# A streaming-encoder block on eight cores: the gate product in bf16 parts, masks made on chip, a finer last block, and head buffers moved

## The chip, the cores and the metric

One Trainium2 chip, all eight cores. Each core works on one of the eight batch elements, with no communication. The time is device microseconds of the slowest core. A program on all eight cores has a slow state in some executions (one die, or both, at a lower granted clock).

TensorE is the matmul engine, VectorE, ScalarE and GpSimd the three elementwise engines. SBUF is the on-chip memory that holds the operands, PSUM the one that TensorE writes its products to (`PS<-SB` in the lines below), in banks; an eviction is the instruction of another engine that reads a product out of PSUM. In the profile's lines they are PE (PEld for its weight loads), DVE, ACT and POOL; SP issues DMAs.

## The reference

For each batch element, x is 2048 tokens by 2048 channels, in float32. Cut to what matters here:

```
h   = rmsnorm(x) * (1 + sc1) + sh1                 # sc1, sh1, ... from c @ w_ada
gk  = log_sigmoid((gk_low @ w_gk2) + b_gk2) / 16   # gk_low: 16 channels of h @ w_in
...                                                # two chunked gated recurrences: 8 heads A, 4 heads B
x   = x + gt1 * (merge of both @ w_o)
h   = rmsnorm(x) * (1 + sc2) + sh2
x   = x + gt2 * ((silu(h @ w_g) * (h @ w_u)) @ w_ffn_out)
out = rmsnorm(x) * final_norm_w
```

The kernel holds channels on partitions and tokens along the free dimension, so the sum of squares over channels is a TensorE product with a matrix of constants, and the final scaling of a token is a multiplication with a tile that is the same on every partition.

## The kernel before

It treats the 2048 tokens in two halves of 1024. A small list scheduler orders all operations with hand-written costs, and each engine then runs its operations in that fixed order. The parts that the change touches:

```
# the gate product of a B head: one float32 product for each 512 tokens
mm([lambda e: e.matmul(p.ap, wgk2.ap[:, i*128:(i+1)*128], gkl[hf].ap, start=True, stop=True)], ...)

# buffers of the heads. Z = 140 KB; the output tiles xres[0..7] lie at Z .. Z+32 KB
r_v  = [sb(194*KB, 4096, BF16), sb(184*KB, 4096, BF16)]
r_B1 = ring(Z + 6*KB, 2, 1024, BF16)
r_B4 = ring(Z + 10*KB, 4, 1024, BF16)     # silu of the output gate
r_rs = ring(202*KB, 2, 512, F32)

# masks: 128 + 4 x 512 float32 columns, by five DMAs in the start
for t_, c0, s_ in ((ident, 0, 2), (m64, 128, 3), (m128, 640, 4), (cm64, 1152, 5), (cm128, 1664, 6)): ...

# the end of the second feed-forward product, for one 128-channel chunk fc
stt(x, p, gt2, x, ALU.mult, ALU.add)                    # VectorE: x += gt2 * psum
act(t_, x, AF.Square)                                   # ScalarE
padd(acc3, acc3, t_)  or  tt(acc3, acc3, t_, ALU.add)   # GpSimd in blocks of 256 (fc < 14), else VectorE
# ... once all 16 chunks of a block are done
norm_finish(acc3, rs3, hf)                              # one float32 product, then Ln and Exp on ScalarE
for fc in range(16):
    stt(x, x, final_norm_w[fc], rs3, ALU.mult, ALU.mult)   # VectorE, then a store

# the last half works its output in blocks
for hf in (0, (512, 256), (768, 256)):                  # (first token, tokens); 0 is 512 tokens
```

## Time and profile before

| | before |
|---|---|
| fast runs | 3772.95 and 3776.08 us |
| slow runs | 3907.97 and 3942.62 us |
| profiled run, span of each core | 3754.0 to 3770.3 us |
| granted TensorE clock of the cores | 0.983 to 0.988 |

The busy line of the profile (busy time, share of the span, instructions; the page that the prediction read has 97% for TensorE, with some hundred matmul records fewer):

```profile
PE 3678.2 (98%) x18414; PEld 1706.8 (45%) x18414; DVE 1334.7 (35%) x2246; ACT 880.1 (23%) x1266; POOL 379.8 (10%) x709
```

TensorE is the limit. What the other engines do costs time only where TensorE has to wait, at the start, or after its last matmul. Four places matter.

The gate product, in the timeline of TensorE (columns of all timeline fences: start, duration, engine, line and operation, operands, and in brackets the idle time before the first instruction of the group and what ended it). Two records are one product, as there are 32 records for 16 float32 products; the last line is two products.

```profile
417.22 1.02 PE L695 MATMUL PS<-SB 128*128 128x512 f32 x2
...
449.29 1.94 PE L695 MATMUL PS<-SB 128*128 128x512 f32 x4
```

The turn from the first half to the second. TensorE stops for 5.66 us: ScalarE could not write the silu of the gate until a store of output had read the same bytes.

```profile
1969.23 7.07 PE L643 MATMUL PS<-SB 128*128 128x512 bf16 x32
...
1980.53 1.29 DVE L380 TENSOR_TENSOR SB<-SB 128x512 bf16<-128x512 bf16 x2 [4.51 <-DMA outT<-SB]
1981.21 1.08 ACT L376 ACTIVATE SB<-PS 128x512 bf16<-128x512 f32 x2 [10.98 <-DMA outT<-SB]
...
1981.96 22.95 PE L643 MATMUL PS<-SB 128*128 128x512 bf16 x96 [5.66 <-ACT SB L376]
```

The start. TensorE makes modulation columns from w_ada_c as it lands; five mask loads (the fence shows four) are issued among the last of them.

```profile
119.86 2.11 POOL L417 DMA_DIRECT2D SB<-cst  x4 [0.64 <-ACT SB L376]
...
147.34 0.54 PE L546 MATMUL PS<-SB 128*128 128x1 bf16 x16 [1.12 <-DMA SB<-w_ada_c]
...
151.93 0.56 PE L546 MATMUL PS<-SB 128*128 128x1 bf16 x16 [4.04 <-DMA SB<-w_ada_c]
```

The end. The list of 128x256 matmuls runs from 3716 us on. The 16 multiplications of the first block of 256 stand in a row on VectorE (7.95 us), the evictions behind them wait, and TensorE stops for 1.80 us. After the last dense matmul (3754.5 us) come GpSimd's additions, the norm product, 16 multiplications and the last store, 15.8 us in all.

```profile
3716.35 19.38 PE L451 MATMUL PS<-SB 128*128 128x256 bf16 x176
...
3739.84 7.95 DVE L400 SCALAR_TENSOR_TENSOR SB<-SB 128x256 f32<-128x256 f32 x16
...
3748.33 6.16 PE L451 MATMUL PS<-SB 128*128 128x256 bf16 x55 [1.80 <-DVE SB L400]
...
3758.47 1.19 PE L508 MATMUL PS<-SB 128*128 128x256 f32 x2 [3.98 <-DVE SB L380]
...
3760.75 6.42 DVE L400 SCALAR_TENSOR_TENSOR SB<-SB 128x256 f32<-128x256 f32 x16 [2.43 <-ACT SB L376]
```

### The profile page before, as it was taken

To read this page: it belongs to the slowest core of one execution; us is meant where nothing else is said; L and a number is where in the kernel's file an instruction comes from. 1 tells how busy PE (TensorE), PEld (TensorE's weight loads), DVE (VectorE), ACT (ScalarE), POOL (GpSimd) and SP (SyncE) were. 2 spreads that over 40 slices of the span, in tenths; PEclk is the share of its full clock that TensorE was granted. 3 is DMA by queue.
4 is the path that set the end of the run, shared out by engine and by line. 5 is a ranking of instruction groups with operands and counts; after the bars stand their busy time and mean duration, and the time that the engine had idled before them with its cause. 6 is when DMAs were issued, how large, how long until landed. Compare 5 with 4: busy or idle time off the path is not lost.

```text
span 3770.1 us, 46917 instructions; the slowest of 8 cores (3754.0 to 3770.3 us)
## 1 busy us (share of the span) xinstructions
PE 3657.4 (97%) x18062; PEld 1707.6 (45%) x18414; DVE 1336.0 (35%) x2246; ACT 880.1 (23%) x1266; POOL 379.8 (10%) x709
## 2 busy tenths in 40 slices
PE   6799999999999999999999999999999999999998
PEld 2344444444444444444444444444444444444445
DVE  2267755532553112231165554321243120211116
ACT  3466323111330000220136643311123000000002
POOL 1111001111011001000000000011101000100002
PEclk7699999999999999999999999999999999999999
DMA  9956558977486545555464433345646454544542
GB/s 195 153 96 108 88 90 129 167 140 141 83 168 116 85 66 86 113 110 88 74 135 100 68 68 68 59 87 99 119 96 116 71 85 71 83 75 69 85 69 90
DMA packets 124540, 377.82 MB, mean 100 GB/s; under 512 B 13601, under 2 KB 20641, under 8 KB 124321
## 3 DMA queue, kind: packets, MB, share of 16 engines
q0 software_dynamic: 97776, 315.44, 50.9%
q1 hardware_dynamic: 26546, 59.36, 5.4%
q8 instruction: 151, 2.47, 0.3%
q14 instruction: 67, 0.55, 0.1%
HBM read 673.35 MB, written 16.78 MB: 183 GB/s over the span
## 4 chain that ended last, share of the span: by engine, by line
PE 92%; DMA 5%; DVE 1%; issue 1%; ACT 1%; SPq 0%; POOL 0%; DVEq 0%; POOLq 0%; ACTq 0%
PE PS L451 82%; PE PS L643 6%; DMA SB<-w_ada_c 1%; DMA SB<-xT 1%; DMA SB<-w_fi_l 1%; DMA SB<-w_ada_l 1%; DVE SB L400 1%; DVE SB L380 1%; ACT SB L376 0%; PE PS L756 0%; PE PS L562 0%; DMA outT<-SB 0%; PE PS L773 0%; PE PS L778 0%; PE PS L695 0%
## 5 line engine op out<-in xcount | busy, mean ns | idle before, releaser
L451 PE MATMUL PS<-SB 128*128 128x512 bf16 (+1 forms) x14869 | 3243.6, 377 | 25.7 <-DMA SB<-w_fi_l 3.2
L451 PEld LDWEIGHTS PS<-SB 128*128 128x128 bf16 x15184 | 1481.4, 98 | 1755.0 <-issue 23.9
L376 ACT ACTIVATE SB<-PS 128x512 f32<-128x512 f32 (+2 forms) x585 | 351.1, 613 | 2266.0 <-PE PS L451 2019.1
L380 DVE TENSOR_TENSOR SB<-PS,SB 128x512 bf16<-128x512 f32 (+1 forms) x256 | 168.2, 657 | 1060.6 <-PE PS L451 947.8
L400 DVE SCALAR_TENSOR_TENSOR SB<-PS,SB 128x512 f32<-128x512 f32 (+2 forms) x416 | 299.6, 727 | 464.3 <-PE PS L451 400.2
L376 ACT ACTIVATE SB<-SB 128x512 f32<-128x512 f32 (+5 forms) x519 | 339.9, 689 | 464.2 <-DVE SB L400 262.2
L380 DVE TENSOR_TENSOR SB<-SB 128x512 f32<-128x512 f32 (+6 forms) x501 | 303.5, 624 | 195.8 <-ACT SB L376 122.3
L400 DVE SCALAR_TENSOR_TENSOR SB<-SB,PS 128x128 f32<-128x128 f32 (+2 forms) x448 | 206.5, 461 | 440.5 <-PE PS L451 400.3
L400 DVE SCALAR_TENSOR_TENSOR SB<-SB 128x2048 bf16<-128x2048 bf16 (+3 forms) x208 | 240.0, 1179 | 62.1 <-DMA SB<-w_ada_l 52.7
L643 PE MATMUL PS<-SB 128*128 128x512 bf16 x999 | 230.1, 382 | 7.5 <-ACT SB L376 5.8
L376 ACT ACT_TABLE_LOAD x146 | 187.3, 1283 | 121.8 <-PE PS L451 75.5
L417 POOL DMA_DIRECT2D SB<-w_fi_l x176 | 92.9, 528 | 1001.3 <-PE PS L451 951.5
L417 POOL DMA_DIRECT2D SB<-w_in_l x144 | 76.1, 529 | 879.8 <-PE PS L451 548.7
L643 PEld LDWEIGHTS PS<-SB 128*128 128x128 bf16 x1024 | 98.7, 98 | 121.2 <-issue 10.0
L417 POOL DMA_DIRECT2D SB<-w_fo_l x128 | 67.6, 528 | 605.0 <-PE PS L451 580.5
L408 DVE CAST SB<-PS 128x512 bf16<-128x512 f32 x64 | 44.1, 690 | 86.5 <-PE PS L643 83.4
L562 PE MATMUL PS<-SB 128*128 128x512 bf16 x86 | 40.8, 610 | 34.0 <-ACT SB L376 33.2
L614 DVE TENSOR_TENSOR_SCAN SB<-SB 128x512 f32<-128x512 bf16 x48 | 58.1, 1218 | 31.6 <-ACT SB L376 31.5
L417 POOL DMA_DIRECT2D SB<-w_ada_l x64 | 33.9, 529 | 172.3 <-PE PS L451 58.3
L525 PE MATMUL PS<-SB 128*128 128x512 f32 x64 | 33.1, 672 | 10.3 <-ACT SB L376 10.3
L408 DVE CAST SB<-SB 128x512 bf16<-128x512 f32 x96 | 40.4, 421 | 0.0
L417 POOL DMA_DIRECT2D SB<-w_v_l x32 | 16.9, 529 | 180.5 <-PE PS L451 99.1
(42 smaller groups left out, 492.9 us busy)
## 6 DMA issues: line engine op xcount, KB each, us to landing
SB<-w_fi_l POOLq DMA_DIRECT2D x176, 512.0 KB, 5.8
SB<-w_in_l POOLq DMA_DIRECT2D x144, 512.0 KB, 6.2
SB<-w_fo_l POOLq DMA_DIRECT2D x128, 352.0 KB, 4.5
SB<-xT SPq DMA_DIRECT2D x64, 512.0 KB, 10.4
SB<-w_ada_l POOLq DMA_DIRECT2D x64, 512.0 KB, 8.4
SB<-w_ada_c POOLq DMA_DIRECT2D x32, 512.0 KB, 19.0
SB<-w_v_l POOLq DMA_DIRECT2D x32, 512.0 KB, 6.1
SB<-w_o_l POOLq DMA_DIRECT2D x32, 512.0 KB, 10.2
```

The lines of the kernel that those rows point to most:

```text
L376: return g.op('act', lambda e: e.activation(out=out.ap, in_=in_.ap, func=func, **kw), reads=[in_] + aps, writes=[out], cost=cost, key=key, ...
L380: return g.op('dve', lambda e: e.tensor_tensor(out=outap if outap is not None else out.ap, in0=in0ap if in0ap is not None else in0.ap, in1 ...
L400: return g.op('dve', lambda e: e.scalar_tensor_tensor(out=out.ap, in0=in0.ap, scalar=v, in1=in1.ap, op0=op0, op1=op1, **kw), reads=[in0, i ...
L408: g.op('dve', lambda e: e.tensor_copy(out=outap if outap is not None else out.ap, in_=inap if inap is not None else in_.ap), reads=[in_], ...
L417: return g.op(q, lambda e: e.dma_start(out=oa, in_=ia), reads=list(reads), writes=list(writes), dsem=sem, nbytes=nbytes, cost=0.6, key=key ...
L451: fns = [(lambda e, k=k: e.matmul(p.ap, w.ap[:, k * 128:(k + 1) * 128], H(acts[k], hf).ap, start=(k == 0), stop=(k == nk - 1))) for k in ks]
L525: mm([lambda e, k=k, hf=hf, q=q: e.matmul(nb[hf].ap, onesD.ap, H(q, hf).ap, start=(k == 0), stop=(k == 15))], [onesD, H(q, hf)], [nb[hf]], ...
L562: mm([lambda e, p=p, j=j, hf=hf, kc=kc: e.matmul(p.ap, ws[j].ap[:, kc * 128:(kc + 1) * 128], H(hT[kc], hf).ap, start=(kc == 0), stop=(kc = ...
L614: g.op('dve', lambda e: e.tensor_tensor_scan(out=dst.ap, data0=mask.ap, data1=src.ap, initial=0.0, op0=ALU.mult, op1=ALU.add), reads=[mask ...
L643: fns = [(lambda e, i=i, j=j, p=p, tb=tb: e.matmul(p.ap, hT[4 * i + j].ap[:, tb * 128:(tb + 1) * 128], ws[i].ap[:, j * 512:(j + 1) * 512], ...
```

## The change

Its intent: shorten TensorE's float32 work (each float32 value of the gate product is split into a bf16 value and a bf16 remainder, and two bf16 products replace one float32 product), take bytes out of the start, take the wait for a store out of the turn, and shorten what follows the last matmul. The core of the diff, with cuts marked by "...":

```diff
-        gkl = [sb(MG + 26 * KB, 512, F32), sb(MG + 28 * KB, 512, F32)]
+        wg_hi, wg_lo = sb(MG + 25 * KB, 512, BF16), sb(MG + 26 * KB, 512, BF16)
+        gkl = [sb(MG + 27 * KB, 512, BF16), sb(MG + 28 * KB, 512, BF16)]    # rows of high and of low parts
...
-                mm([... e.matmul(p.ap, wgk2.ap[:, i * 128:(i + 1) * 128], gkl[hf].ap, start=True, stop=True)],
+                mm([... e.matmul(p.ap, w_.ap[:, i * 128:(i + 1) * 128], gkl[hf].ap, start=(n_ == 0), stop=(n_ == 1))
+                    for n_, w_ in enumerate((wg_hi, wg_lo))], ...)
...
-        r_v = [sb(194 * KB, 4096, BF16), sb(184 * KB, 4096, BF16)]
+        r_v = [sb(194 * KB, 4096, BF16), sb(Z + 10 * KB, 4096, BF16)]
-        r_B1 = ring(Z + 6 * KB, 2, 1024, BF16)
-        r_B4 = ring(Z + 10 * KB, 4, 1024, BF16)
+        r_B1 = ring(202 * KB, 2, 1024, BF16)
+        r_B4 = ring(184 * KB, 4, 1024, BF16)
-        r_rs = ring(202 * KB, 2, 512, F32)
+        r_rs = ring(Z + 6 * KB, 2, 512, F32)
...
-    cst_d = din("cst", [128, 128 + 4 * 512])
+    cst_d = din("cst", [128, 384])          # cm64, cm128 by memset; m64, m128 broadcast over four blocks
...
+                    elif q == 3:            # the last half
+                        a_ = H((acc3, acc4)[fc % 2], hf)
+                        t_ = q3().cols(0, width(hf)) if fc > 1 else a_
+                        act(t_, x, AF.Square)
+                        act(x, x, AF.Copy, scale=sm(SM_NF + fc), key=2.5)      # final_norm_w, on ScalarE
+                        if fc > 1:          # odd chunks on GpSimd, even ones on VectorE
+                            (padd if fc % 2 else lambda o_, a, b: tt(o_, a, b, ALU.add))(a_, a_, t_)
...
+                norm_finish([acc3, acc4], rs3, hf)                             # two float32 products
+                for f0 in ((4, 12, 0, 8) if n == 512 else (12, 0, 4, 8)):      # four chunks at a time
+                    pl = f0 == 12 or (n == 512 and f0 == 4)
+                    ...
+                    g.op('pool' if pl else 'dve', lambda e, ...: e.tensor_tensor(out=base, in0=base, in1=rsb, op=ALU.mult), ...)
...
-                    for hf in (0, (512, 256), (768, 256)):
+                    for hf in (0, (512, 256), (768, 128), (896, 128)):
```

## The prediction

> **What bounds it now.** TensorE: in the busy table 97% of 3770 us. Its 15,000 dense 128x512 bf16 matmuls stand 0.216 us apart in the timeline, at a granted clock of 0.985. Its waits by cause sum to only about 21 us after 157 us; before that it waits for xT, then w_ada_c. So three things pay: less matmul time, the start, the tail after the last matmul. VectorE (35%), ScalarE (23%) and GpSimd (10%) have room everywhere but at the end.
>
> **What the change does.**
>
> 1. Gate product. In the timeline a pair of float32 records of the gate matmul takes 0.86 to 0.91 us; 32 records are 16 products. Two bf16 products take 2 x 0.216 = 0.43 us. Saving 0.46 x 16 = about 7 us on TensorE, where it has no idle. "TensorE: Matmul & The Clock Gate" (the Trainium skill, Weight-path perf modes) ties fast weight load to non-float32 types; the trace agrees (loads of 190 ns in float32, 98 in bf16).
>
> 2. Head buffers. At the turn of the two 1024-token halves the timeline shows TensorE idle from 1976.3 to 1982.0 us: two silu evictions waited 11 us for an output DMA, since their target overlays output tiles. Afterwards nothing in the first head's front does. Saving 5 to 5.7 us.
>
> 3. Masks. Five cst loads (1.1 MB of HBM reads) are issued at 120 to 123 us amid the last w_ada_c loads, for which TensorE waits until 151.9. From 126.3 to 151.8 about 8 MB landed, 0.32 MB/us; 0.92 MB less is about 3 us.
>
> 4. Tail. The last dense matmul ends near 3754.5, the span at 3770.3: 15.8 us of GpSimd additions to 3757, norm, 16 multiplications of 128x256 on VectorE (6.4 us), last store (3 us). TensorE also stood 1.8 us at 3746.5, behind the multiplications of the block before. After, for 128 tokens, estimated from the durations shown: eviction, square, addition 1.5; norm 1.7 to 2; three multiplications of 128x512 on VectorE 2.1; last store 2.5 to 3: 8 to 9 us. 128-wide matmuls stand 0.056 us apart, so two blocks of 128 (19.7 us) cost TensorE little more than one of 256 (19.2). Against it: norm sums take two float32 products (+0.9, +0.5, +0.3 us), and in the 128 blocks ScalarE (two instructions of an estimated 0.31 us per 0.62 us) and VectorE (about 9.5 of 9.9 us) are at their limit, an estimated lag of 1 to 2 us. Net 5 to 7 us.
>
> The broadcast mask costs VectorE the same 0.69 us; the silu ring, cut to two, is reused every 6.9 us only.
>
> **Sum.** 7 + 5.5 + 3 + 6 = about 21 us, 0.6%. From fast runs of 3773 to 3776: **3753 us**, range 3743 to 3764. Faster by over 2%: 0.01; within 2%: 0.97; slower: 0.02.
>
> **What would show each step.** Gate: 32 bf16 records 0.216 us apart. Turn: no TensorE idle over 1 us after the second half's first front, no wait for an output DMA. Masks: the last w_ada_c wait ends near 149 us. Tail: 8 to 10 us from last dense matmul to end, no stall in the 256 block.
>
> **What would make it wrong.** GpSimd's wide multiplications (4 x 512 columns, an estimated 4 to 6 us each) block its additions and, through the ring of squares, ScalarE and the evictions. VectorE is slowed beside GpSimd (its 128x512 multiplications went from 0.74 to 0.82-0.99 us). The start may be limited by the ring of eight w_ada_c tiles, not bytes: then term 3 is nothing. The list schedule shifts, adding small stalls. A slow-state run (3908 was seen) as the median.

## The result, and the profile after

| | before | after |
|---|---|---|
| fast runs | 3772.95, 3776.08 us | 3762.99 to 3764.37 us (four) |
| slow runs | 3907.97, 3942.62 us | 3891.29, 3911.76 us |
| profiled run, span of each core | 3754.0 to 3770.3 us | 3747.3 to 3763.2 us |

The ratio is 0.9972, with a 95% interval from 0.9948 to 0.9996: about 10.6 us less, half of the 21 us that the prediction summed. A ratio here is the mean time of one kernel's fast runs over that of the other's of the same rounds, so it is not quite the ratio of medians. Of the four fast runs one lies at the very top of the predicted range of 3743 to 3764 and three just above it.

Cores differ by up to 20 us within one execution, so one core's trace is a poor yardstick for single terms. The next table gives the mean over all eight cores of each profiled execution, worked out from the times in the traces: the start of the first value product (after the start-up), the first 128x256 dense matmul (where the last 512 tokens begin to be worked in smaller blocks), the end of the last dense matmul, and the span.

| mean of 8 cores, us | before | after | difference |
|---|---|---|---|
| start to the first value product | 176.3 | 173.5 | -2.8 |
| from there to the first 128x256 matmul | 3532.7 | 3520.9 | -11.9 |
| from there to the end of the last dense matmul | 38.1 | 50.6 | +12.5 |
| of it TensorE waiting | 1.8 | 9.4 | +7.6 |
| from there to the end of the span | 15.7 | 11.3 | -4.4 |
| span | 3762.9 | 3756.2 | -6.6 |

Three terms arrived. The loss is in the last 65 us. The long middle row is the least exact: within one execution it differs from core to core by up to 13 us (3526.2 to 3539.0 before), and five kernels that differ only near or after its end (the change, dve_only, psum_sq, two256 and pool_narrow below) have means of 3518.9 to 3522.5 us. A mean there is good to about 2 us, so an agreement to a tenth is luck.

The busy line after:

```profile
PE 3674.3 (98%) x18600; PEld 1710.7 (45%) x18600; DVE 1343.1 (36%) x2246; ACT 912.9 (24%) x1352; POOL 397.6 (11%) x712
```

The gate product: one line is now two products of two bf16 records, four records spaced 0.216 us.

```profile
443.32 1.03 PE L703 MATMUL PS<-SB 128*128 128x512 bf16 x4
```

The turn: the value products run without a break. VectorE still waits 2.68 us for a store (a state tile that overlays an output tile), and nothing waits for VectorE there.

```profile
1963.49 26.71 PE L648 MATMUL PS<-SB 128*128 128x512 bf16 x123
...
1977.49 0.23 DVE L410 COPY SB<-SB 128x128 f32<-128x128 f32 x1 [2.68 <-DMA outT<-SB]
```

The start: one mask load, and the last wait for w_ada_c ends at 148.1 us, not 151.9.

```profile
118.87 0.53 POOL L419 DMA_DIRECT2D SB<-cst  x1 [0.64 <-ACT SB L378]
...
148.14 0.56 PE L551 MATMUL PS<-SB 128*128 128x1 bf16 x16 [1.81 <-DMA SB<-w_ada_c]
```

The end, on core 1 (the slowest):

```profile
3701.29 9.33 PE L453 MATMUL PS<-SB 128*128 128x256 bf16 x84
...
3704.35 2.40 DVE L1001 TENSOR_TENSOR SB<-SB 128x2048 f32<-128x2048 f32 x1 [0.34 <-ACT SB L378]
3704.56 6.55 POOL L1001 TENSOR_TENSOR SB<-SB 128x2048 f32<-128x2048 f32 x1
3706.67 4.73 DVE L382 TENSOR_TENSOR SB<-SB 128x256 f32<-128x256 f32 x1
...
3711.94 4.96 PE L453 MATMUL PS<-SB 128*128 128x256 bf16 x44 [1.31 <-DVE SB L402]
...
3713.19 6.55 POOL L1001 TENSOR_TENSOR SB<-SB 128x2048 f32<-128x2048 f32 x1
3715.31 4.72 DVE L382 TENSOR_TENSOR SB<-SB 128x256 f32<-128x256 f32 x1
...
3720.57 9.98 PE L453 MATMUL PS<-SB 128*128 128x256 bf16 x136 [3.66 <-DVE SB L402]
...
3735.03 4.00 DVE L1001 TENSOR_TENSOR SB<-SB 128x1024 f32<-128x1024 f32 x3
...
3739.64 4.85 PE L453 MATMUL PS<-SB 128*128 128x128 bf16 x44 [4.10 <-DVE SB L402]
...
3754.61 1.11 PE L512 MATMUL PS<-SB 128*128 128x128 f32 x4 [2.89 <-POOL SB L388]
...
3756.59 2.96 DVE L1001 TENSOR_TENSOR SB<-SB 128x512 f32<-128x512 f32 x3 [2.89 <-ACT SB L378]
3756.63 1.77 POOL L1001 TENSOR_TENSOR SB<-SB 128x512 f32<-128x512 f32 x1 [2.28 <-ACT SB L378]
```

Read the VectorE lines first. An addition of 128x256 (L382) is listed with 4.73 us, and another with 4.72; the same instruction takes 0.43 us elsewhere in this trace. Its end falls 0.29 us after the end of the GpSimd multiplication of 128x2048 (L1001) that was running: 3706.67 + 4.73 = 3711.40, and 3704.56 + 6.55 = 3711.11; the second pair ends at 3720.03 and 3719.74. The wait is inside the listed duration, so the line shows no idle time and the busy table counts it as work. The other direction is there too: GpSimd's 6.55 us begin while VectorE runs its own multiplication of 128x2048, which ends at 3706.75; from there it is 4.36 us. While the addition stands, the evictions behind it on VectorE stand as well, the PSUM banks fill, and TensorE stops for 1.31 and 3.66 us. A third stop of 4.10 us follows VectorE's three multiplications of 128x1024 in a row (4.00 us from 3735.03), ahead of which another addition waited for GpSimd (2.26 us from 3732.84).

The same wait already stands in the trace before the change, on a small scale:

```profile
3721.43 0.73 POOL L386 TENSOR_TENSOR SB<-SB 128x256 f32<-128x256 f32 x1 [0.58 <-ACT SB L376]
...
3721.72 0.99 DVE L400 SCALAR_TENSOR_TENSOR SB<-SB 128x512 f32<-128x512 f32 x1
```

VectorE's multiplication of 128x512 takes 0.74 us alone. Here it ends at 3722.71, 0.55 us after the end of GpSimd's addition at 3722.16. The next three that meet an addition of GpSimd end 0.54 to 0.56 us after it as well: each waited for it.

The stops cost more than their length. In the table of stretches (columns: stretch, its length, busy time and instructions of PE, PEld, DVE, ACT and POOL, granted TensorE clock, DMA share, GB/s):

```profile
3717.00:3720.50 3.50, 0.00 (x0) 0.00 (x0) 3.50 (x3) 0.00 (x0) 3.50 (x2) 1.00 0.61 228
3720.50:3722.00 1.50, 1.43 (x7) 1.02 (x8) 1.50 (x5) 1.25 (x4) 0.84 (x2) 0.52 0.86 328
3722.00:3724.00 2.00, 2.00 (x17) 1.72 (x15) 1.81 (x6) 1.31 (x3) 0.00 (x0) 0.51 0.79 287
3724.00:3726.00 2.00, 2.00 (x39) 2.00 (x37) 1.60 (x5) 1.52 (x4) 0.00 (x0) 1.00 0.01 4
3737.50:3739.60 2.10, 0.00 (x0) 0.00 (x0) 2.10 (x5) 0.00 (x0) 0.00 (x0) 0.53 1.01 339
3739.60:3742.00 2.40, 2.36 (x23) 2.39 (x24) 1.69 (x7) 2.20 (x9) 0.91 (x2) 0.50 1.02 340
3742.00:3744.30 2.30, 2.30 (x25) 2.30 (x22) 0.70 (x2) 0.62 (x3) 0.46 (x1) 0.50 0.71 244
```

After each long stop the granted clock is 0.50 to 0.52 for some 3.4 to 4.7 us: 44 matmuls of 128x128 took 4.85 us from 3739.64, 0.110 us each, where 88 of them took 5.08 us (0.058 each) in the next block. "TensorE: Matmul & The Clock Gate" (the Trainium skill, What's actually happening) describes this: the array falls to half its clock after an idle window of about 3.4 us and needs about as long a busy one to return. The traces agree in part: on all eight cores the stops of 3.7 and 4.1 us were followed by half clock, and the stop of 1.8 us before the change was not (granted clock 1.00 after it). But a stop did not have to last 3.4 us. In the runs below half clock also followed stops of 2.9 us (dve_only, six of eight cores), 3.1 us (psum_sq, six) and 3.2 us (pool_narrow, seven), and on two cores one of 2.0 us (old_tail), after which 55 matmuls of 128x256 took 7.83 us instead of 6.16. What decides between the cores was not tested.

After the last dense matmul, 11.5 us on this core: TensorE waits 2.89 us for GpSimd's last addition, behind a row of ten instructions on ScalarE; the multiplications take 2.96 us instead of 2.1, beside GpSimd's 1.77.

### The profile page after: what moved, and what is told of

Same layout as the page of the kernel before. It is cut to its first block, busy times and chain, and to the rows that moved or that the text cites. A ratio compares the mean times of both kernels' runs of the same rounds, so it can differ in the third digit from the quotient of the medians.

```text
span 3763.2 us, 47979 instructions; the slowest of 8 cores (3747.3 to 3763.2 us)
## 1 busy us (share of the span) xinstructions
PE 3674.3 (98%) x18600; PEld 1710.7 (45%) x18600; DVE 1343.1 (36%) x2246; ACT 912.9 (24%) x1352; POOL 397.6 (11%) x712
## 4 chain that ended last, share of the span: by engine, by line
PE 93%; DMA 4%; DVE 1%; issue 1%; SPq 0%; ACT 0%; POOL 0%; DVEq 0%; ACTq 0%; POOLq 0%
PE PS L453 84%; PE PS L648 6%; DMA SB<-w_ada_c 2%; DMA SB<-w_fi_l 1%; DMA SB<-xT 1%; DMA SB<-w_ada_l 1%; DVE SB L382 1%; PE PS L765 0%; DVE SB L402 0%; PE PS L782 0%; PE PS L788 0%; SPq L419 0%; PE PS L799 0%; PE PS L512 0%; PE PS L733 0%
## 5 line engine op out<-in xcount | busy, mean ns | idle before, releaser
L453 PE MATMUL PS<-SB 128*128 128x512 bf16 (+2 forms) x15360 | 3272.0, 375 | 17.1 <-DVE SB L402 9.9
L382 DVE TENSOR_TENSOR SB<-PS,SB 128x512 bf16<-128x512 f32 (+1 forms) x256 | 168.1, 657 | 1060.7 <-PE PS L453 947.3
L378 ACT ACTIVATE SB<-SB 128x512 f32<-128x512 f32 (+6 forms) x600 | 368.8, 654 | 462.8 <-DVE SB L402 250.8
L402 DVE SCALAR_TENSOR_TENSOR SB<-PS,SB 128x512 f32<-128x512 f32 (+3 forms) x432 | 301.9, 707 | 461.4 <-PE PS L453 395.1
L382 DVE TENSOR_TENSOR SB<-SB 128x512 f32<-128x512 f32 (+7 forms) x512 | 316.4, 636 | 196.3 <-ACT SB L378 109.5
L402 DVE SCALAR_TENSOR_TENSOR SB<-SB,PS 128x128 f32<-128x128 f32 (+3 forms) x452 | 209.4, 464 | 424.0 <-PE PS L453 383.9
L402 DVE SCALAR_TENSOR_TENSOR SB<-SB 128x2048 bf16<-128x2048 bf16 (+2 forms) x160 | 213.2, 1350 | 75.3 <-DMA SB<-w_ada_l 68.7
L551 PE MATMUL PS<-SB 128*128 128x1 bf16 x512 | 17.7, 165 | 18.7 <-DMA SB<-w_ada_c 18.1
```

Of the source, the lines that this page charges most:

```text
L378: return g.op('act', lambda e: e.activation(out=out.ap, in_=in_.ap, func=func, **kw), reads=[in_] + aps, writes=[out], cost=cost, key=key, ...
L382: return g.op('dve', lambda e: e.tensor_tensor(out=outap if outap is not None else out.ap, in0=in0ap if in0ap is not None else in0.ap, in1 ...
L402: return g.op('dve', lambda e: e.scalar_tensor_tensor(out=out.ap, in0=in0.ap, scalar=v, in1=in1.ap, op0=op0, op1=op1, **kw), reads=[in0, i ...
L453: fns = [(lambda e, k=k: e.matmul(p.ap, w.ap[:, k * 128:(k + 1) * 128], H(acts[k], hf).ap, start=(k == 0), stop=(k == nk - 1))) for k in ks]
L551: mm([lambda e, p=p, w=w, k=k: e.matmul(p.ap[:, 0:1], w.ap[:, k * 128:(k + 1) * 128], ccol.ap[:, k:k + 1], start=(k == 0), stop=(k == 15)) ...
```

## The experiments

The theory (A): wide two-operand multiplications on GpSimd hold a port to SBUF that VectorE's additions of two SBUF operands need, for the whole GpSimd instruction; this turns the end from a gain into a loss. The SBUF page of the Trainium skill ("SBUF — State Buffer", Who interferes with whom) says it: a VectorE instruction with two SBUF inputs contends with a GpSimd instruction that reads SBUF, and one with at most one SBUF input, outside the two-port modes, does not. The traces agree: beside a wide GpSimd multiplication an addition is listed with 4.73 us in the change, and with 0.41 us in psum_sq, where one operand is in PSUM. Rivals: (B) the blocks of 128 are too fine for ScalarE and VectorE; (C) the multiplications are too wide for the evictions, wherever they run.

All twelve runs are correct against the reference. Each is given with its ratio to the kernel before on the same chip and its fast runs. The intervals of dve_only, psum_sq and pool_narrow overlap with that of the change (0.9948 to 0.9996), so the case for the cause rests mainly on their traces. Their fast runs (3753.5 to 3761.9 us) do lie below all those of the change (3763.0 to 3764.4 us), though in the rounds of these runs the kernel before was 1 to 3 us slower. "Blocks" is the mean over eight cores from the first 128x256 matmul to the end of the last dense matmul, "tail" from there to the end, as in the table above (before: 38.1 + 15.7; after: 50.6 + 11.3).

### old_tail: the other three parts alone

```diff
  in the after kernel: squares, sums, final multiplications, the blocks 512, 256, 256
  and the buffer rings of this part as before
```

> The changed kernel with its tail (squares, sums, final multiplications, blocks of 512, 256, 256) put back as before; gate, masks and head buffers stay changed. Theory A (the new tail is the only loss: GpSimd's wide multiplications hold the SBUF port that VectorE's additions of two SBUF operands need): the other three terms bring 16 to 17 us, so about 3757.5 us in a fast run (kernel before 3774, changed 3764.2), and 15.8 us from the last dense matmul to the end. If the tail is not the loss, it stays at 3764 or goes up.

Ratio 0.9945 (0.9929 to 0.9962); fast runs 3755.4, 3756.0 and 3757.9 us, kernel before 3777.0 in the mean: 20.6 us less. In the mean over cores the start is 2.3 us shorter than before, the middle 14.1, blocks and tail 38.7 + 15.2, the span 16.4. So the three other parts bring what was forecast or a little more, and the new tail costs against the old one 8.0 us in blocks and tail, or 9.7 us in the mean span, which has the scatter of the middle in it. On core 1, where both profiled runs happen to begin the norm of the 512 block at 3699.6 to 3699.7 us, TensorE's waits from 3680 us on are (us in total, times, longest), in old_tail:

```profile
PE PS L512 <- DVE SB L382: 4.0, 1, 4.0
PE PS L453 <- DVE SB L402: 2.0, 1, 2.0
```

and in the after kernel:

```profile
PE PS L453 <- DVE SB L402: 9.4, 4, 4.1
PE PS L512 <- POOL SB L388: 2.9, 1, 2.9
```

In this core's trace the sum closes: from that norm to the last dense matmul is 13.0 us longer (7.4 us more waiting for evictions; about 4.1 us at half clock, which is half of 3.4 and of 4.8 us; about 1.9 us of additional norm products), the rest 4.3 us shorter, together the 8.6 us between spans of 3754.6 and 3763.2 (the parts add up to within half a microsecond).

### dve_only: no multiplication on GpSimd

```diff
-                    pl = f0 == 12 or (n == 512 and f0 == 4)
+                    pl = False
```

> The changed kernel with all final multiplications on VectorE, none on GpSimd. Theory A: the two VectorE additions of 4.7 us in the block of 256 shrink to 0.43 us and TensorE's stalls of 1.3 and 3.7 us there go; the stall of 4.1 us in the first block of 128 shrinks by about 2 or stays, as the wide multiplications still stand in a row before the evictions; 3757 to 3761 us. Rival B (the blocks of 128 overload ScalarE and VectorE): 3763 to 3766. Rival C (the multiplications are too wide for the evictions wherever they run): VectorE has 4.4 us more of them, so slower than 3764.

Ratio 0.9951 (0.9938 to 0.9965); five fast runs, 3755.5 to 3761.9 us. Blocks and tail 42.9 + 10.4: 8.6 us less than after, although VectorE has more to do. No addition is longer than 0.94 us. TensorE waits 4.7 us, the longest 2.9 us behind four multiplications of 128x1024 in a row (5.41 us). Rival C as the main cause falls; as a smaller part it stays.

### psum_sq: the additions' second operand in PSUM

```diff
-                        t_ = q3().cols(0, width(hf)) if fc > 1 else a_
+                        t_ = (q3() if fc % 2 else qps()).cols(0, width(hf)) if fc > 1 else a_     # qps() is PSUM bank 7
...
```

> The changed kernel with the squares of the even chunks written to a PSUM bank, so that VectorE's additions read one SBUF and one PSUM operand; GpSimd's multiplications are as wide as before. Theory A: the additions no longer wait (0.4 us each beside a GpSimd multiplication of 4.4 to 6.6 us), the stalls in the block of 256 go: 3756 to 3760 us. Rivals B and C: no difference, 3763 to 3765.

Ratio 0.9954 (0.9939 to 0.9969); four fast runs, 3757.9 to 3761.5 us. Blocks and tail 42.0 + 11.7, 8.2 us less than after. This is the cleanest test, for GpSimd's instructions are as wide as in the after kernel:

```profile
3709.16 6.58 POOL L1007 TENSOR_TENSOR SB<-SB 128x2048 f32<-128x2048 f32 x1
3711.27 0.41 DVE L382 TENSOR_TENSOR SB<-SB,PS 128x256 f32<-128x256 f32 x1
...
3713.32 4.56 DVE L1007 TENSOR_TENSOR SB<-SB 128x2048 f32<-128x2048 f32 x1
...
3718.43 4.55 POOL L1007 TENSOR_TENSOR SB<-SB 128x2048 f32<-128x2048 f32 x1
...
3718.92 0.41 DVE L382 TENSOR_TENSOR SB<-SB,PS 128x256 f32<-128x256 f32 x1
```

Beside GpSimd's multiplications of 6.58 and 4.55 us the additions now take 0.41 us. VectorE's own multiplication of two SBUF operands, between them, still takes 4.56 us instead of 2.3: it waits. So it is the second SBUF operand that is blocked, not VectorE as such. (The even squares also leave the ring of SBUF buffers to the odd ones, which was not tested apart; it does not bear on how long an addition takes.) The remaining stop (3.1 us) again follows the three multiplications in the first block of 128.

### two256: the fine split undone

```diff
-                    for hf in (0, (512, 256), (768, 128), (896, 128)):
+                    for hf in (0, (512, 256), (768, 256)):
```

> The changed kernel with blocks 512, 256, 256 instead of 512, 256, 128, 128. Theory A: both 4.7 us additions and the stalls of about 5 us in the first block of 256 stay; no stall of 4.1 us with its cold clock (2.4 us more) in a block of 128, but about 4 us more after the last dense matmul; 3761 to 3766 us. Rival B: the loss is the split, so 3758 us or less.

Ratio 0.9965 (0.9949 to 0.9982); four fast runs, 3762.4 to 3765.2 us. Blocks and tail 42.7 + 15.8. The two additions of 4.73 and 4.72 us and the stops of 1.32 and 3.67 us are there as in the after kernel. Rival B falls as the main cause: without the split the loss against old_tail is still 4.6 us in blocks and tail and 7 us in the fast runs. As a smaller part it stays: with GpSimd in the way, the split makes blocks and tail 3.4 us longer (61.9 against 58.5), through the stop in the block of 128 and the half clock after it; the ratios of the two kernels (0.9965 and 0.9972) do not tell them apart.

### gate_only, heads_only, masks_only: one part each, on the kernel before

```diff
  gate_only:  wg_hi, wg_lo, the split gkl, two bf16 products;  nothing else
  heads_only: r_v, r_B1, r_B4, r_rs at their new places;       nothing else
  masks_only: cst of 384 columns, memsets, broadcast masks;    nothing else
```

> The kernel before with the gate product alone as bf16 high and low parts. Expected 7 us less than before (16 products at 0.89 us become 16 at 0.43 us) in fast runs, all of it between the first value product and the last 512 tokens, averaged over the eight cores. Rival: float32 weight loads also hid other work, or the extra split delays the first gate head, then less than 5.

> The kernel before with the head buffers moved alone. Expected 5 to 6 us less than before, as TensorE's idle of 5.7 us at the turn of the halves and the 11 us wait of ScalarE for an output DMA go. Rival: the wait moves to the value evictions on VectorE (busy with the output multiplications there), then 0 to 3 us.

> The kernel before with the masks made on chip alone. Expected 3 us less than before at the first value product, averaged over the eight cores, if bytes bound the start; nothing if the ring of eight w_ada_c tiles does.

- gate_only: only one of its six runs was fast (3766.0 us, against a mean of 3773.2 before), so there is no interval. Its profiled run was slow on one die; on the four cores of the undisturbed die the first 128x256 matmul comes at 3702.6 us in the mean, 7.0 us earlier than the 3709.6 of the same cores before, 0.5 us of it already at the first value product. With the scatter of the middle this supports the forecast but does not measure it to a tenth; the spacing of the records does that better.
- heads_only: ratio 0.9981 (0.9965 to 0.9998), four fast runs, mean 3766.6 us: 6.6 us less. The middle is 6.2 us shorter in the mean over cores.
- masks_only: ratio 0.9988 (0.9968 to 1.0008), two fast runs, mean 3768.7 us, not clear of noise in the time. In the trace the first value product comes 3.0 us earlier in the mean over cores. That it is the bytes, and not the four fewer DMA issues, was not tested apart.

### pe_sum: sums on TensorE, all multiplications on VectorE

```diff
...
+                        act(t_, x, AF.Square)                 # t_ now bf16
+                        mm([lambda e: e.matmul(nb.ap, onesDb.ap, t_.ap, start=(fc == 0), stop=(fc == 15))], ...)
-                        (padd if fc % 2 else ...)(a_, a_, t_)
-                norm_finish([acc3, acc4], rs3, hf)
+                act(rs3, nb, AF.Ln, bias=EPS); act(rs3, rs3, AF.Exp, scale=-0.5)
...                                                          # all final multiplications on 'dve', f0 = 0, 4, 8, 12
```

> The changed kernel with the squares of the last 1024 tokens written in bf16 and summed by TensorE into a PSUM bank, no additions on VectorE or GpSimd, and all final multiplications on VectorE (four chunks each). Theory A and VectorE's load as the second cause: no stall in the 256 block, at most 2 us in the first 128 block, 7 to 8.5 us after the last dense matmul; TensorE pays 16 products of 0.216, 0.107, 0.056 and 0.056 us, 7 us in all, instead of 4 us of float32 ones. 3 to 5 us less than old_tail, so 3751 to 3754 where the kernel before takes 3777. If VectorE's load is not the second cause, no better than dve_only.

Ratio 0.9939 (0.9923 to 0.9956); three fast runs, 3749.4 to 3751.1 us, 23 us less than before. TensorE's own work at the end grows, and yet blocks and tail are 43.7 + 8.0. The tail of 8.0 us is the one that the prediction had estimated (8 to 9). A stop of 1.1 us remains behind three multiplications in a row. Since dve_only has no wide GpSimd instruction either, what pe_sum gains on it (1.6 us of blocks and tail) comes from the additions on two engines, the float32 products, what stood behind them and the order of the multiplications together; these were not separated. Expected were 3 to 5 us less than old_tail: the ratios give 2 us, with intervals that overlap, the mean spans 4.8 us (3746.5 and 3741.7).

### pool_narrow: the same GpSimd work in quarter-width instructions

```diff
-                    g.op('pool', ... out=base, in0=base, in1=rsb ...)            # 4 x n columns
+                    for x in xs:
+                        g.op('pool', ... out=x.ap, in0=x.ap, in1=H(rs3, hf).ap ...)  # n columns
```

> The changed kernel with GpSimd's final multiplications cut into single chunks (512, 256 or 128 columns each instead of four times that), the same work on the same engine. If a VectorE addition waits for the GpSimd instruction in progress to end (Theory A in its narrow form), additions wait at most 1.3 us each, TensorE's stalls in the block of 256 fall from 5 us to under 1, and the time falls by 3 to 6 us to about that of dve_only. If only the amount of GpSimd work counts, the stalls stay.

Ratio 0.9947 (0.9929 to 0.9964); three fast runs, 3753.5 to 3758.0 us. Blocks and tail 42.0 + 11.6.

```profile
3703.19 5.96 POOL L1002 TENSOR_TENSOR SB<-SB 128x512 f32<-128x512 f32 x3
3705.30 1.48 DVE L382 TENSOR_TENSOR SB<-SB 128x256 f32<-128x256 f32 x1
...
3711.84 1.45 POOL L1002 TENSOR_TENSOR SB<-SB 128x512 f32<-128x512 f32 x1
...
3712.48 1.09 DVE L382 TENSOR_TENSOR SB<-SB 128x256 f32<-128x256 f32 x1
...
3714.12 1.27 POOL L1002 TENSOR_TENSOR SB<-SB 128x512 f32<-128x512 f32 x1
3714.68 1.00 DVE L382 TENSOR_TENSOR SB<-SB 128x256 f32<-128x256 f32 x1
```

GpSimd's instructions here take 1.27 to 1.45 us each (the first of the three in the first line waited for VectorE), and the additions that meet one are listed with 1.00 to 1.48 us, waiting to its end (3711.84 + 1.45 = 3713.29; the addition ends at 3713.57). One is over the 1.3 us expected. No stop of TensorE remains among the dense matmuls of the block of 256; 0.5 us is left before its norm product. So the work on GpSimd is harmless there, and its width was the fault. The time fell by more than the 3 to 6 us expected: by the ratios, about 9 us against the change. The stop of 3.2 us in the first block of 128 stays, behind three multiplications on VectorE that take 4.54 us.

### pe_sum_256, pe_stag, pe_mix: what the split is worth, and a better kernel

```diff
  pe_sum_256: pe_sum with blocks 512, 256, 256
  pe_stag:    pe_sum; the key of the final multiplication f0 is 3 + 0.0095 * n * (f0 // 4), so that evictions come between
  pe_mix:     pe_stag; the 512 block's squares in float32, added on VectorE, one float32 norm product
```

> pe_sum with blocks 512, 256, 256. Shows what the split into 128 is worth when GpSimd is out of the way: after the last dense matmul about 3.5 us more than the 8.1 of pe_sum (multiplications 2 x as wide, 2.2 us more; store, norm and eviction about 1 more), blocks about 1 us less, so 2 to 3 us slower than pe_sum. If the split is a loss in itself, faster than pe_sum.

> pe_sum with its final multiplications spread among the evictions (one after every two to four) instead of three in a row. If the order on VectorE caused the remaining stall of 1.1 us and ScalarE's backlog, 1 to 2 us faster than pe_sum, no stall in the blocks of 128; else the same.

> pe_stag with the sum of the 512 block as before the change (VectorE additions and one float32 product). TensorE pays 0.9 us there instead of 3.5, so 2 to 2.6 us faster than pe_stag, if nothing else waits.

- pe_sum_256: ratio 0.9941 (0.9926 to 0.9955), three fast runs, mean 3753.6 us. Blocks and tail 42.1 + 11.5, 1.9 us more than pe_sum. The finer split is worth about 2 us once nothing stands in its way. The times alone do not tell the two apart.
- pe_stag: five runs counted as fast, four of 3748.6 to 3750.2 us and one of 3772.8, which widens the interval (ratio 0.9942, 0.9922 to 0.9962). No wait of TensorE over 0.3 us is left, and blocks and tail are 42.5 + 8.0, 1.2 us less than pe_sum: as expected in the trace, unresolved in the time.
- pe_mix: ratio 0.9924 (0.9911 to 0.9936); five fast runs, 3744.9 to 3750.5 us, mean 3747.1 against 3775.9 before. Blocks and tail 39.4 + 8.2. It is 29 us faster than the kernel before and beats the changed kernel's ratio by 0.48%. From 3690 us on, all of TensorE's waits in its profiled trace are:

```profile
PE PS L989 <- ACT SB L379: 0.7, 2, 0.4
```

## Why the prediction was wrong

- **What bounds it: right.** Everything that took time from TensorE showed in the time.
- **Term 1, gate, about 7 us: right.** The bf16 records stand 0.216 us apart, as the sum assumed; 7.0 us on four undisturbed cores, within their scatter.
- **Term 2, turn, 5 to 5.7 us: right, a little low.** 6.2 us in the mean over cores, which the scatter of the middle does not tell from 5.7; the idle of 5.7 us is gone. The sign that it named, no wait for an output DMA, was not met to the letter: VectorE waits 2.68 us for one, at no cost.
- **Term 3, masks, about 3 us: right.** 2.8 us in the change, 3.0 alone; the last w_ada_c wait ended at 148 us, "near 149".
- **Term 4, tail, "Net 5 to 7 us": wrong in sign, and the step that failed.** The new tail costs 8.0 us of blocks and tail against the old one (old_tail against after: 53.9 and 61.9 us; 9.7 us in the mean span, 3746.5 and 3756.2). The terms of that sum: the last dense matmul to the end was to be 8 to 9 us and was 11.3; the lag of ScalarE and VectorE was to be 1 to 2 us, and TensorE waited 9.4 us in the blocks, 7.6 more than before, and ran at half clock after two of the stops. "No stall in the 256 block" was the sign, and there were two.
- **Why it failed.** The prediction named both pieces as risks: GpSimd's wide multiplications, of which it said that they block "its additions", GpSimd's own, and VectorE "slowed beside GpSimd", from 0.74 to 0.82-0.99 us. It carried neither into the sum as a wait of VectorE, and did not put the two together. The slower multiplications had waited for a GpSimd addition of only 0.73 us to end, as the lines above show. An estimate follows from its own numbers: an instruction of an estimated 4 to 6 us on GpSimd would hold a VectorE addition for up to that long, and the six PSUM banks in turn, one filled every 1.2 us, give 7 us of room, less what VectorE already owes. psum_sq, dve_only and pool_narrow each remove the wait by another means and each recover about 8 us of blocks and tail.
- **The second fault.** Without the wait the new tail would still only have equalled the old (53.3 to 53.7 us of blocks and tail against 53.9), where 5 to 7 us were forecast. The prediction allowed VectorE 9.5 of 9.9 us in a block of 128 and no order; multiplications stood three or four in a row ahead of the evictions. pe_mix, which takes sums off VectorE and GpSimd and puts evictions between the multiplications, gets 6.3 us less than the old tail: the forecast was within reach of the idea, not of this form of it. From dve_only (53.3 us of blocks and tail) to pe_mix (47.6) the steps are 1.6 us for the sums on TensorE (pe_sum), 1.2 us for the order (pe_stag), and 2.9 us for the 512 block's sum back on VectorE, where VectorE has the time (pe_mix). Each step is one profiled run, a mean of eight cores.

## What to carry to other kernels

Work given to GpSimd beside a busy VectorE is not free: here, where both read two SBUF operands, one waited for the other's whole instruction (4.73 us listed for an addition of 0.43 us), and the profile shows that wait as busy time, so compare an instruction's listed duration with its usual one. Keep GpSimd's instructions narrow, or give VectorE a PSUM operand, or move the sum to TensorE. TensorE's two long stops (3.66 and 4.10 us on core 1) were paid about one and a half times, since it restarted at half clock and lost some 4.1 us more. And the order of wide operations and evictions on one engine matters as well as their sum: it was worth 1.2 us from pe_sum to pe_stag, in the traces alone.

## What the Trainium skill lacked or had wrong

- "GPSIMD Engine Reference" (Specifications) says only that its SBUF interfaces are shared with VectorE, with contention if VectorE has two SBUF inputs or is in a two-port mode; that the wait lasts for the whole instruction stands on another page, "SBUF — State Buffer". Here: an addition of 0.43 us listed with 4.73 us beside a GpSimd multiplication of 128x2048, and with 1.00 to 1.48 us when that was cut to 128x512. Nothing was wrong; the prediction did not use it.
- "SBUF — State Buffer" does not say how the wait of a VectorE or GpSimd instruction appears in a profile: inside the busy time of the waiting instruction, with no idle time before it (additions of 4.73 and 4.72 us, GpSimd multiplications of 6.55 us that were 4.36 us of work).
- "TensorE: Matmul & The Clock Gate" (What's actually happening) calls the cost of the return from half clock under 1% of a typical kernel, which holds here too, yet two stops of 3.7 and 4.1 us near the end cost about 4.1 us more at half clock on core 1, about as much as the tail became shorter (4.4 us). The idle window of about 3.4 us that it gives is not a safe limit here: half clock also followed stops of 2.9 us (six of eight cores of dve_only), 3.1 us (six, psum_sq), 3.2 us (seven, pool_narrow) and 2.0 us (two, old_tail), and none of the stops of 1.0 to 1.8 us of dense matmuls in the last 90 us of these runs.
